# Running products in a PSUM bank: keep formed in place of the scores, one two-bank PSUM tile split in two, and a new order

## The chip, the cores and the metric

The kernel runs on one core of a Trainium2 chip. The metric is the device time of one execution in microseconds. Several engines work side by side, each with a queue of its own that it takes strictly in order: TensorE (PE) for matrix products, with its weight loads (PEld), VectorE (DVE), ScalarE (ACT), GpSimd (POOL) and SyncE (SP), which issues the DMAs. Products land in PSUM, eight banks of 512 fp32 columns in each of 128 partitions. Inputs of the other engines lie in SBUF or, except for POOL, in PSUM.

## The reference, cut to what matters

Two layers work on a sequence of 512 tokens with 1024 channels. The even layer joins a gated linear recurrence and a block attention (softmax); the odd one joins a stick-breaking attention (8 heads of 64 channels) and a state-space model. Each begins with an RMS norm and an adaptive modulation (adaLN) and ends with an output projection. The change is in the stick-breaking attention and around it:

```python
def stick_breaking_attention(q, k, v):
    for blk in range(t_ // SB_QBLOCK):                 # 4 blocks of 128 queries
        q0 = blk * SB_QBLOCK
        end = q0 + SB_QBLOCK
        z = jnp.einsum('bhqd,bhkd->bhqk', q[:, :, q0:end], k[:, :, :end]) * scale
        strict = jnp.arange(end)[None, :] < qpos[:, None]
        log_beta = jax.nn.log_sigmoid(z)
        log_keep = jnp.where(strict, jax.nn.log_sigmoid(-z), 0.0)
        later = lax.cumsum(log_keep, axis=3, reverse=True) - log_keep
        w = jnp.where(strict, jnp.exp(log_beta + later), 0.0)
        outs.append(jnp.einsum('bhqk,bhkd->bhqd', w, v[:, :, :end]))
```

A weight is thus sigmoid(z) times the product of sigmoid(-z) over all later keys.

## The kernel before, in words

The program is first recorded, then ordered, then emitted. `Rec.add` notes each operation with its operands; `Rec.cost` gives it an estimated duration; `Rec.schedule` places the operations one after another on the engine queues, by a priority (`prio`, the PE time recorded so far) that the tables `SHIFTS` shift by ranges of operation numbers (nanoseconds, negative is earlier). Operations recorded with `either` may run on DVE or on POOL or ACT; the planner gives them to the engine on which they end sooner, after the bias that `CHOICE` adds for ranges of numbers. `emit` then writes the instructions in that order, and the tile framework adds the waits between engines by what each instruction reads and writes. All instructions carry one line number, 603, so rows are told apart by the names of their tiles.

Matrix products with 512 columns are formed from a high and a low part of each factor (`mm3`: three products). A weight tile `wst` comes by DMA, ACT (or POOL) casts it to `wh`, and DVE or POOL forms the remainder `wl`.

At the start x comes in eight tiles; ACT squares them, DVE adds the squares into an accumulator (in the trace `t`), and `rms` sums its columns on PE (`ones,t`), forms the mean on DVE (`ms`), a power on POOL, a diagonal on DVE (`diag`), a product on PE, and a copy `rb`. `modulate` then forms `hs` (DVE), `hh` (ACT) and `hl` (DVE) for each of eight blocks of channels, with a scale and shift that DVE's dot products over `aw` deliver. Eight products of x with itself into a bank that nobody reads (`warm`) stand in PE's queue as well.

PSUM's banks are shared by tags: `pj` banks 0 to 3, `ps` 4 and 5, `pt` 6, `pv` 7, and in the attentions `fj` 0 and 1, `as` 2 to 4 (scores), `at` 5 and 6 (transposed weights), `av` 7 (values). `pw`, a row of 1024 columns that the dot products read early in the kernel, takes banks 6 and 7 together. For it, banks 6 and 7 are one PSUM tile of 1024 columns, and `pt`, `pv`, `at` and `av` are views of it.

In `attend`, per pair of query blocks and one or two heads: `both` spreads q into `qd` by DMA, `scores` forms the scores in an `as` bank (rows `k,qd`), `weights_moba` (even layer) or `weights_stick` (odd layer) forms the weights in SBUF, PE transposes them into an `at` bank (rows `ident,w` and `ident,u`), ACT casts that to `wth` and DVE forms the remainder `wtl`. `values` multiplies with v into the `av` bank (rows `wth,v`) and then ACT and DVE read the halves of that bank into `ya` (even) or `yb` (odd), twice each. In `weights_stick`, `u` and `keep` are two SBUF tiles of the tag `u2o`, which has six slots; five of them share memory with other temporaries. There are 24 tiles in the odd layer, 8 with two heads and 16 with one, of 128, 256, 384 and 512 columns per head, and 32 scans. While the attentions run, the output projections and, in the odd layer, a gated product (`glu`, tile `zval`) fill PE's queue.

The state-space model is worked in four quarters between the odd layer's projections; it transposes through `pt` and multiplies into `pv`.

Of the kernel before, what the change touches and what calls it, by code (L numbers as in the profile page):

```python
# [11 lines left out]
F32 = mybir.dt.float32  # L12
# [3 lines left out]
OP = mybir.AluOpType  # L16
AX = mybir.AxisListType
PSUM = bass.MemoryType.PSUM
# [164 lines left out]
class Eng:  # L183
# [8 lines left out]


SHIFTS = (
# [11 lines left out]
)  # L206
CHOICE = (
# [3 lines left out]
)  # L211


class Rec:
# [191 lines left out]
    def schedule(self, key=None):  # L406
# [14 lines left out]
        last = {}  # L421
# [13 lines left out]
        dma_free, act_set, order = 0.0, None, []  # L435

        port, port_free, tile = None, 0.0, None
        slot, speed, rows = 0, 1.0, 0.0

        def arrive(op):  # L440
            for e in [a[0] for a in op.alts] or [op.eng]:
# [35 lines left out]
        while left:  # L477
            best = None
            for e in self.ENGINES:
                now = clock[e]  # L480
                pick = None
                for op in cand[e].values():
                    r = op.ready
                    got = ()
                    if op.new:
                        s = place(op)
# [14 lines left out]
                    start = max(now, r)  # L501
                    sw = 0
                    if e == "scalar" and op.aset and act_set not in op.aset:
                        sw = 1
                    k = (start if start > now + (self.dma_window if e == "sync" else self.window) else now,
                         key[op.n] + (4000.0 if sw else 0.0), op.n)
# [8 lines left out]
            _, op, sw, got, start, e = best  # L515
# [73 lines left out]
    def emit(self, nc, base, psum, preload):  # L589
        def real(v):  # L590
            return v.real() if isinstance(v, View) else v
        for op in self.order:
            if isinstance(op, str):
                preload(op)
                continue
            for b in op.new:
                if b.psum:
                    b.ap = psum[self.banks[b.tag][b.slot] if b.tag != "pw" else 8]
                    continue
                off = base + 4 * self.memory[b.tag][0][b.slot]  # L600
                b.ap = nc.alloc_sbuf_tensor_at("%s_%d" % (b.name, op.n), list(b.shape), b.dtype, offset=off).ap()
            kw = {k: real(v) for k, v in op.kw.items() if k != "nbytes"}
            op.ins = getattr(getattr(nc, op.eng), op.method)(*[real(a) for a in op.args], **kw)  # L603
# [74 lines left out]
class Hybrid:  # L678
# [7 lines left out]
    def bank(self, tag):  # L686
        return self.R.buf([128, 512], F32, tag)
# [55 lines left out]
    def setup(self):  # L743
# [24 lines left out]
        row = R.buf([1, D], F32, "crow")  # L768
        self.act(row, crow, "Tanh", scale=0.5)
        R.vector.scalar_tensor_tensor(out=row, in0=row, scalar=1.0, in1=crow, op0=OP.add, op1=OP.mult)  # L770
        self.crow = R.buf([128, D], F32, "pw")
        for i in range(2):
            h = slice(i * 512, i * 512 + 512)
            R.tensor.matmul(self.crow[:, h], lhsT=self.ones[0:1], rhs=row[:, h], start=True, stop=True)

    def load_late(self):
        R = self.R
# [79 lines left out]
            self.either_tt(sq, sq, acc, OP.add)  # L857
        return sq

    def rms(self, acc, bank):  # L860

        R, n = self.R, acc.shape[1]
        r = n // 128
        p = self.bank(bank)
        for i in range(r):
            R.tensor.matmul(p[:, i:i + 1], lhsT=acc[:, i * 128:i * 128 + 128], rhs=self.ones[:, 0:1], start=True, stop=True)
        ms = R.buf([128, 4], F32, "st", "ms")[:, 0:r]
        R.vector.tensor_scalar(ms, p[:, 0:r], 1.0 / D, EPS, op0=OP.mult, op1=OP.add)
        R.gpsimd.tensor_tensor(out=ms, in0=ms, in1=self.mhalf[:, 40:40 + r], op=OP.pow)
        diag = R.buf([128, r, 128], F32, "t2" if n == 512 else "sq256", "diag")  # L870
        R.vector.tensor_tensor(out=diag, in0=self.ident[:, None, :].to_broadcast([128, r, 128]),
                               in1=ms[:, :, None].to_broadcast([128, r, 128]), op=OP.mult)
        p = self.bank(bank)[:, 0:n]
        diag = diag.rearrange("p r e -> p (r e)")
        R.tensor.matmul(p, lhsT=self.ones, rhs=diag, start=True, stop=True)
        return p

    def new_h(self):
# [215 lines left out]
    def weights_stick(self, s, g, n):  # L1094

        R = self.R
        w, keep = (R.buf([128, g, n], F32, "u2o", x) for x in ("u", "keep"))
        self.act(keep, s, "Sigmoid", scale=-1.0)
        self.act(w, s, "Sigmoid")
        for j in range(g):  # L1100

            z = keep[:, j, 1:n][:, ::-1]
            R.vector.tensor_tensor_scan(out=z, data0=z, data1=z, initial=1.0, op0=OP.mult, op1=OP.min)
        R.vector.tensor_tensor(out=w[:, :, 0:n - 1], in0=w[:, :, 0:n - 1], in1=keep[:, :, 1:n], op=OP.mult)
        return w

    def attend(self, q, k, v, sg, mix, weights, scratch, mask, groups):
# [94 lines left out]
    def even(self):  # L1202
# [6 lines left out]
            R.sync.dma_start(xt, A['x_t'][k * 128:k * 128 + 128, :])  # L1209
            self.x.append(xt)  # L1210
        aw0 = self.ada_load(0)

        warm = self.bank("ps")
        for k in range(8):
            R.tensor.matmul(warm[:, 0:256], lhsT=self.x[k][:, 0:128], rhs=self.x[k][:, 0:256], start=True, stop=True)
        for k in range(8):
            acc = self.square(k, everything, acc)
        ab = R.buf([128, 3, 8], F32, "ab")
        self.new_h()
        rb = R.buf([128, 512], F32, "t2", "rb")  # L1220
        R.scalar.copy(rb, self.rms(acc, "ps"))
        xl = []

        def evac_xl(b, p):
# [425 lines left out]
@with_exitstack  # L1650
def hybrid_kernel(ctx, tc, *aps):
    nc = tc.nc
    m = Hybrid(dict(zip(_NAMES, aps)), aps[len(_NAMES)])
    R = m.record()
    R.schedule()
    pool = ctx.enter_context(tc.tile_pool(name="psum", bufs=1, space=PSUM))
    psum = [pool.tile([128, 512], F32, name="bank%d" % i) for i in range(6)]
    two = pool.tile([128, 1024], F32, name="bank67")
    psum += [two[:, 0:512], two[:, 512:1024], two]
    ctx.enter_context(tc.manual_schedule())  # L1660
    R.emit(nc, -(-nc.sbuf_base // 32) * 32, psum, nc.scalar.preload_act_table_set)
    return m


# [17 lines left out]
```

## Time and profile before

| | us |
|---|---|
| median of 3 runs | 568.76 (567.86 to 572.07) |
| the profiled execution, its own time | 569.02 |
| span of the profiled execution | 567.2 |
| PE busy, share of the span | 526.4 (93%) |
| DVE busy | 461.8 (81%) |
| ACT busy | 285.6 (50%) |
| POOL busy | 156.1 (28%) |

The span runs from the first to the last instruction of the profiled execution; 1.8 us of its time lie around it. Busy times of PE are sums over pipelined products, so 93% doesn't mean that PE works at its peak. The stages follow one another with overlap: start and first projection to 64 us, the even layer's projections and recurrence to about 200, its attention and output to about 290, the odd layer's projections with the state-space quarters to about 445, its attention and output to the end. Times in rows are microseconds from the span's start unless marked ns.

### The profile page before, as it was taken

What the parts mean: (1) busy time and instruction counts of PE and PEld (TensorE: products, weight loads), DVE (VectorE), ACT (ScalarE), POOL (GpSimd) and SP (SyncE); (2) the same over time, 40 slices, a digit from 0 to 9 for tenths busy, and PEclk for the clock granted to TensorE, in tenths of its full rate; (3) what the DMA queues carried; (4) which work ended last, traced back from release to release, by engine and by line L of the source; (5) the groups of instructions that cost most, each with busy time, mean ns of one, the idle gap of its engine ahead of it and who ended that gap; (6) DMA issues with size and microseconds to landing.
All of it is one profiled execution on the core that took longest, in us unless ns stands there. A gap on an engine that the chain in (4) does not pass through costs nothing.

```text
span 567.2 us, 8032 instructions
## 1 busy us (share of the span) xinstructions
PE 526.4 (93%) x2762; PEld 426.3 (75%) x2762; DVE 461.8 (81%) x917; ACT 285.6 (50%) x551; POOL 156.1 (28%) x164
## 2 busy tenths in 40 slices
PE   6697999999999999899999998989999988999997
PEld 3465688667777777788779987867877876776787
DVE  5799998999978988879787666767865799998973
ACT  5424532484645867764652327246254675845320
POOL 0000231233435304454799000200041502212100
PEclk9999999999999999999999999999999999999999
DMA  8985599981234634311023321212025343312122
GB/s 297 404 293 184 200 342 318 373 281 55 84 112 142 157 112 141 107 43 49 27 74 106 117 75 37 75 39 68 27 82 163 91 119 90 116 28 68 44 102 86
DMA packets 45755, 75.59 MB, mean 133 GB/s; under 512 B 4241, under 2 KB 28945, under 8 KB 44690
## 3 DMA queue, kind: packets, MB, share of 16 engines
q1 hardware_dynamic: 45714, 75.08, 40.9%
q8 instruction: 22, 0.36, 0.3%
q14 instruction: 19, 0.16, 0.1%
HBM read 64.57 MB, written 2.10 MB: 118 GB/s over the span
## 4 chain that ended last, share of the span: by engine, by line
PE 49%; DVE 29%; ACT 10%; DMA 4%; issue 4%; POOL 2%; SPq 0%; DVEq 0%; ACTq 0%; POOLq 0%
PE bank L603 49%; DVE aw L603 4%; DVE wl L603 3%; DMA aw<-in_od_ada_t_dram 2%; DVE keep L603 2%; DVE wtl L603 2%; DVE hs L603 2%; POOL qms L603 2%; DVE hl L603 2%; ACT wpr_wpi_opr_opi L603 1%; DVE u L603 1%; DMA wst<-in_od_w_out_dram 1%; ACT wth L603 1%; DVE x L603 1%; DVE yb L603 1%
## 5 line engine op out<-in xcount | busy, mean ns | idle before, releaser
L603 ACT CAST wh<-wst 128x1024 fp32r<-128x1024 f32 x58 | 60.9, 1050 | 79.5 <-PE bank L603 49.1
L603 PE MATMUL bank<-wl,hh 128*128 128x512 f32 x224 | 88.2, 397 | 1.8 <-DVE wl L603 1.8
L603 PE MATMUL bank<-wh,hl 128*128 128x512 f32 x224 | 87.7, 396 | 0.2 <-DVE hl L603 0.2
L603 PE MATMUL bank<-wh,hh 128*128 128x512 f32 x224 | 87.1, 398 | 0.4
L603 DVE TENSOR_TENSOR wl<-wst,wh 128x1024 fp32r<-128x1024 f32 x53 | 67.7, 1282 | 15.0 <-ACT wh L603 14.6
L603 PE MATMUL bank<-hh,wh 128*128 128x512 f32 x160 | 61.1, 409 | 8.4 <-ACT hh L603 8.4
L603 PE MATMUL bank<-hl,wh 128*128 128x512 f32 x160 | 63.5, 404 | 0.0
L603 POOL TENSOR_TENSOR wl<-wst,wh 128x1024 fp32r<-128x1024 f32 x15 | 36.3, 2425 | 93.3 <-ACT wh L603 83.4
L603 PE MATMUL bank<-hh,wl 128*128 128x512 f32 x160 | 61.5, 393 | 0.0
L603 PEld LDWEIGHTS bank<-wl,hh 128*128 128x128 f32 x224 | 46.0, 205 | 10.6 <-DVE wl L603 3.1
L603 PEld LDWEIGHTS bank<-wh,hh 128*128 128x128 f32 x224 | 45.7, 205 | 9.7 <-issue 1.2
L603 PE MATMUL bank<-q,wh 128*128 128x256 f32 x256 | 50.6, 289 | 2.1 <-DVE q L603 0.7
L603 PEld LDWEIGHTS bank<-wh,hl 128*128 128x128 f32 x224 | 46.0, 205 | 8.2 <-DVE hl L603 0.8
L603 POOL TENSOR_TENSOR qms<-qms,derived 128x8 f32<-128x8 f32 x16 | 29.3, 1837 | 62.6 <-DVE qms L603 61.2
L603 PEld LDWEIGHTS bank<-hh,wh 128*128 128x128 f32 x160 | 29.9, 191 | 19.5 <-ACT hh L603 13.0
L603 PEld LDWEIGHTS bank<-q,wh 128*128 128x128 f32 x256 | 40.6, 190 | 4.4 <-DVE x L603 2.2
L603 DVE CUSTOM_DVE_ANT_0 aw<-aw,bank,lcols 128x1024 f32<-128x1024 f32 x32 | 40.5, 1273 | 2.4 <-DMA aw<-in_od_ada_t_dram 2.4
L603 PEld LDWEIGHTS bank<-hl,wh 128*128 128x128 f32 x160 | 30.6, 191 | 8.4 <-DVE hl L603 1.5
L603 PE MATMUL bank<-q,wl 128*128 128x256 f32 x128 | 36.2, 288 | 0.0
L603 PEld LDWEIGHTS bank<-hh,wl 128*128 128x128 f32 x160 | 30.1, 188 | 6.6 <-issue 0.7
L603 PE MATMUL bank<-k,qd 128*128 128x512 f32 (+3 forms) x128 | 34.1, 326 | 0.0
L603 ACT CAST wth<-bank 128x512 fp32r<-128x512 f32 (+2 forms) x48 | 24.0, 516 | 18.1 <-PE bank L603 15.1
(213 smaller groups left out, 1199.1 us busy)
## 6 DMA issues: line engine op xcount, KB each, us to landing
aw<-in_od_ada_t_dram SPq DMA_DIRECT2D x24, 512.0 KB, 5.9
aw<-in_ev_ada_t_dram SPq DMA_DIRECT2D x8, 1024.0 KB, 8.8
wst<-in_od_w_in_dram SPq DMA_DIRECT2D x16, 512.0 KB, 3.6
wst<-in_ev_w_in_dram SPq DMA_DIRECT2D x12, 512.0 KB, 7.2
wst<-in_ev_w_in_dram SPq DMA_DIRECT2D x24, 256.0 KB, 3.5
aw<-in_ev_gate_t_dram SPq DMA_DIRECT2D x8, 512.0 KB, 4.4
wst<-in_ev_w_out_dram SPq DMA_DIRECT2D x8, 512.0 KB, 4.2
qd<-q SPq DMA_DIRECT2D x32, 128.0 KB, 2.8
```

Of the source, the lines that this page charges most:

```text
L603: op.ins = getattr(getattr(nc, op.eng), op.method)(*[real(a) for a in op.args], **kw)
```

## The change

Four things change. In `weights_stick`, `keep` is no longer a tile: the second sigmoid overwrites the scores in their PSUM bank, the scan runs there in place with a column of ones (broadcast from SBUF) as its second input, and the product reads it there. The two sigmoids change places. The two-bank PSUM tile is kept only for `pw`, in a pool that is closed when bank 6 or 7 is first asked for; after that they are two tiles of one bank each. The eight `warm` products over x are removed; two products of constants in `setup` and two in the even layer's first `rms` are added. The tables `SHIFTS` and `CHOICE` are new, with 37 and 9 entries where there were 53 and 14, and the planner takes PE's clock as low at the start (`speed`). From the first `rms` on, an operation's number is 4 less than before.

```diff
 SHIFTS = (
-    (2018, 2019, 10518), (3854, 3894, 10778), (1287, 1298, 5289), (30, 597, 1554), (1147, 1634, 3396),
...
-    (4262, 4303, 13376), (1439, 1476, -789),
+    (3043, 3052, 8774), (1018, 1022, 3924), (1599, 1710, 5502), (1584, 1598, 4615), (2497, 2513, -6921),
+    (3049, 3072, -26458), (3231, 3550, 2254), (486, 517, 1193), (2346, 2401, -24614), (3853, 3885, 7046),
...
+    (519, 670, -2481), (2126, 2133, 2353), (3624, 3661, 1122), (1122, 1215, -435), (1644, 1663, -16577),
+    (3005, 3006, 23610), (815, 1188, 1028), (1837, 1847, 518), (3071, 3134, -9248), (702, 707, -7222),
...
 )
...
-        slot, speed, rows = 0, 1.0, 0.0
+        slot, speed, rows = 0, 0.5, 0.0
...
-                    b.ap = psum[self.banks[b.tag][b.slot] if b.tag != "pw" else 8]
+                    b.ap = psum(8 if b.tag == "pw" else self.banks[b.tag][b.slot])
...
+        warm = self.bank("ps")
+        R.tensor.matmul(warm, lhsT=self.ones, rhs=self.moba_mask, start=True, stop=True)
         self.crow = R.buf([128, D], F32, "pw")
         for i in range(2):
             h = slice(i * 512, i * 512 + 512)
             R.tensor.matmul(self.crow[:, h], lhsT=self.ones[0:1], rhs=row[:, h], start=True, stop=True)
+        R.tensor.matmul(warm, lhsT=self.ones, rhs=self.moba_mask, start=True, stop=True)
...
-    def rms(self, acc, bank):
+    def rms(self, acc, bank, warm=None):
...
+        if warm is not None:
+            R.tensor.matmul(warm, lhsT=self.ones, rhs=acc, start=True, stop=True)
...
+        if warm is not None:
+            R.tensor.matmul(warm, lhsT=self.ones, rhs=diag, start=True, stop=True)
...
-        w, keep = (R.buf([128, g, n], F32, "u2o", x) for x in ("u", "keep"))
-        self.act(keep, s, "Sigmoid", scale=-1.0)
+        w = R.buf([128, g, n], F32, "u2o", "u")
         self.act(w, s, "Sigmoid")
+        self.act(s, s, "Sigmoid", scale=-1.0)
         for j in range(g):
 
-            z = keep[:, j, 1:n][:, ::-1]
-            R.vector.tensor_tensor_scan(out=z, data0=z, data1=z, initial=1.0, op0=OP.mult, op1=OP.min)
-        R.vector.tensor_tensor(out=w[:, :, 0:n - 1], in0=w[:, :, 0:n - 1], in1=keep[:, :, 1:n], op=OP.mult)
+            z = s[:, j, 1:n][:, ::-1]
+            R.vector.tensor_tensor_scan(out=z, data0=z, data1=self.ones[:, 0:1].to_broadcast([128, n - 1]), initial=1.0,
+                                        op0=OP.mult, op1=OP.min)
+        R.vector.tensor_tensor(out=w[:, :, 0:n - 1], in0=w[:, :, 0:n - 1], in1=s[:, :, 1:n], op=OP.mult)
         return w
...
-        warm = self.bank("ps")
-        for k in range(8):
-            R.tensor.matmul(warm[:, 0:256], lhsT=self.x[k][:, 0:128], rhs=self.x[k][:, 0:256], start=True, stop=True)
...
-        R.scalar.copy(rb, self.rms(acc, "ps"))
+        R.scalar.copy(rb, self.rms(acc, "ps", self.bank("ps")))
...
-    psum = [pool.tile([128, 512], F32, name="bank%d" % i) for i in range(6)]
-    two = pool.tile([128, 1024], F32, name="bank67")
-    psum += [two[:, 0:512], two[:, 512:1024], two]
+    banks = {i: pool.tile([128, 512], F32, name="bank%d" % i) for i in range(6)}
+    first = ExitStack()
+    banks[8] = first.enter_context(tc.tile_pool(name="two", bufs=1, space=PSUM)).tile([128, 1024], F32, name="two")
+
+    def bank(i):
+
+        if i not in banks:
+            first.close()
+            pool = ctx.enter_context(tc.tile_pool(name="last", bufs=1, space=PSUM))
+            banks.update({j: pool.tile([128, 512], F32, name="bank%d" % j) for j in (6, 7)})
+        return banks[i]
```

## Rows read from the trace of the kernel before

**Rows 1.** Windows: stretch, its length, busy us of PE, PEld, DVE, ACT, POOL, clock, DMA.
```profile
22.00:64.00 42.00, 34.35 (x132) 24.99 (x133) 39.87 (x103) 14.53 (x22) 2.40 (x1) 1.00 0.70 250
200.00:262.00 62.00, 55.76 (x375) 48.08 (x373) 50.27 (x137) 41.56 (x106) 26.00 (x34) 1.00 0.30 86
480.00:540.00 60.00, 56.39 (x315) 44.79 (x313) 56.61 (x83) 34.32 (x72) 12.12 (x12) 1.00 0.22 65
```

**Rows 2.** Timeline of PE, 10 to 26 us: start, length, engine, line, what [idle before].
```profile
10.90 4.64 PE L603 MATMUL bank<-x 128*128 128x256 f32 x10
15.33 1.71 PE L603 MATMUL bank<-ones,t 128*128 128x1 f32 x8
19.13 2.07 PE L603 MATMUL bank<-diag,ones 128*128 128x512 f32 x2 [2.10 <-DVE diag L603]
23.42 2.07 PE L603 MATMUL bank<-hh,wh 128*128 128x512 f32 x4 [2.21 <-ACT hh L603]
```

**Rows 3.** Timeline of DVE in the same stretch.
```profile
10.81 1.49 DVE L603 TENSOR_TENSOR t<-t,t 128x512 f32<-128x512 f32 x2 [0.69 <-ACT t L603]
13.30 1.28 DVE L603 CUSTOM_DVE_ANT_0 aw<-aw,bank,ecols 128x1024 f32<-128x1024 f32 x1 [1.00 <-DMA aw<-in_ev_ada_t_dram]
...
17.07 0.16 DVE L603 TENSOR_SCALAR ms<-bank 128x4 f32<-128x4 f32 x1 [1.09 <-PE bank L603]
18.38 0.69 DVE L603 TENSOR_TENSOR diag<-ident,ms 128x512 f32<-128x512 f32 x1 [1.15 <-POOL ms L603]
...
21.86 0.75 DVE L603 SCALAR_TENSOR_TENSOR hs<-x,ab,rb 128x512 f32<-128x512 f32 x1 [0.51 <-ACT rb L603]
```

**Rows 4.** Who waited for whom, 200 to 262 us: total us, times, longest.
```profile
DVE ya L603 <- ACT wth L603: 3.4, 4, 1.9
...
ACT ya L603 <- DVE wtl L603: 2.5, 4, 0.9
...
ACT wth L603 <- DVE ya L603: 2.1, 2, 1.1
...
PE bank L603 <- ACT ya L603: 1.4, 3, 0.5
```

**Rows 5.** Timeline of DVE and PE, two of these waits.
```profile
225.72 0.42 DVE L603 SCALAR_TENSOR_TENSOR ya<-bank,ya 64x256 f32<-64x256 f32 x1 [0.30 <-ACT wth L603]
...
230.46 0.44 PE L603 MATMUL bank<-ident,w 128*128 128x128 f32 x2 [0.47 <-ACT ya L603]
```

**Rows 6.** Who waited for whom, 345 to 400 us.
```profile
PE bank L603 <- ACT kx_ug_yt L603: 2.7, 4, 1.6
```

**Rows 7.** Groups by shape, whole span: count | busy us, mean ns | idle before.
```profile
L603 DVE TENSOR_TENSOR wtl<-bank,wth 128x512 fp32r<-128x512 f32 x24 | 16.4, 684 | 1.1 <-PE bank L603 0.7 <-ACT wth L603 0.2
...
L603 DVE TENSOR_TENSOR_SCAN keep<-keep 128x511 f32<-128x511 f32 x8 | 10.2, 1277 | 0.0
...
L603 ACT ACTIVATE keep<-bank 128x512 f32<-128x512 f32 x12 | 7.2, 599 | 2.4 <-DVE u L603 1.8 <-PE bank L603 0.3
...
L603 DVE TENSOR_TENSOR u<-u,keep 128x511 f32<-128x511 f32 x8 | 5.5, 683 | 0.0
```

**Rows 8.** Timeline of PE and DVE, one tile of 512 columns of the odd attention.
```profile
489.45 0.62 PE L603 MATMUL bank<-k,qd 128*128 128x512 f32 x2
...
494.85 1.76 DVE L603 TENSOR_TENSOR_SCAN keep<-keep 128x511 f32<-128x511 f32 x1
...
498.01 0.69 DVE L603 TENSOR_TENSOR u<-u,keep 128x511 f32<-128x511 f32 x1
```

**Rows 9.** Waits and DVE groups, 445 to 540 us; POOL's timeline; the tile zval (min/median/max ns).
```profile
ACT keep L603 <- DVE u L603: 4.9, 7, 1.3
...
L603 DVE TENSOR_TENSOR wl<-wst,wh 128x1024 fp32r<-128x1024 f32 x9 | 10.9, 1211 | 0.2 <-ACT wh L603 0.2
...
474.35 2.50 POOL L603 TENSOR_TENSOR wl<-wst,wh 128x1024 fp32r<-128x1024 f32 x1
...
L603 DVE SCALAR_TENSOR_TENSOR zval<-zval,sgs x4: 681/950/2807, 463.1 to 498.6; 128x512 f32<-128x512 f32 x4
```

More of the change, by code (lines that the diff above doesn't have):

```diff
@@ L194 @@
 SHIFTS = (
[11 rows of a table removed]
[8 rows of a table added]
 )
 CHOICE = (
[3 rows of a table removed]
+    (2594, 2626, -1252), (438, 517, 666), (2023, 2030, 493), (2111, 2197, -4241), (634, 736, 2066), (3652, 3707, 728),
+    (3792, 3897, 3536), (2146, 2211, 3242), (2437, 2552, 1411),
 )
@@ L1656, in hybrid_kernel @@
     pool = ctx.enter_context(tc.tile_pool(name="psum", bufs=1, space=PSUM))
-    psum = [pool.tile([128, 512], F32, name="bank%d" % i) for i in range(6)]
-    two = pool.tile([128, 1024], F32, name="bank67")
-    psum += [two[:, 0:512], two[:, 512:1024], two]
+    banks = {i: pool.tile([128, 512], F32, name="bank%d" % i) for i in range(6)}
[7 more added lines that the diff above has]
+        return banks[i]
     ctx.enter_context(tc.manual_schedule())
-    R.emit(nc, -(-nc.sbuf_base // 32) * 32, psum, nc.scalar.preload_act_table_set)
+    R.emit(nc, -(-nc.sbuf_base // 32) * 32, bank, nc.scalar.preload_act_table_set)
     return m
```

16 rows, old and new, of tables (CHOICE, SHIFTS) are left out of this document.

## The prediction

> **What bounds the kernel now.** I read the windows of the span first, then the timeline of the first 25 us, then who waited for whom in the attention stages, then single rows of the timeline. The windows [rows 1] show two different regimes. From 22 to 64 us VectorE (DVE) is busy 39.87 of 42.00 us: the adaLN dot products set the pace, whatever TensorE (PE) does. In the even layer's attention (200 to 262) no engine is full: PE is busy 55.76 of 62.00 us, DVE 50.27, ScalarE (ACT) 41.56, so the end is set by engines handing work to each other. In the odd layer's attention (480 to 540) DVE is again close to the limit, 56.61 of 60.00 us, with PE at 56.39. Outside of these PE streams 512-column matmuls back to back; the change doesn't touch that work, so its worth must come from the start, from the two attentions and from the state-space quarters.
>
> **Start: the warm-up matmuls move.** Before, eight fp32 matmuls of 256 columns over x stand in PE's queue, and the five that are left at 10.90 occupy PE until 15.5 us [rows 2]. The sum of squares that they have nothing to do with is complete on DVE at 10.81 + 1.49 = 12.30 us [rows 3], but its column sums start on PE only at 15.33 [rows 2]. DVE then waits for them and for what follows: 1.09 us before ms at 17.07, 1.15 before diag at 18.38, 0.51 before hs at 21.86 [rows 3], 2.75 us in all. Removing the x matmuls lets the column sums start at 12.3, 3.0 us earlier. From ms to hs the old chain takes 21.86 - 17.07 = 4.79 us; it now starts at about 14.1, but hs also needs the scale of block 0, whose data lands at 13.30 [rows 3] and whose two dots hold DVE until about 16.0, so diag waits for DVE until 16.0 instead of 15.4. That puts hs at 16.0 + (21.86 - 18.38) = 19.5, a gain of 2.4 us. From there DVE is the limit up to 64 us [rows 1], so the head start is passed on; DMA is at 0.70 of its time in that stretch, enough in hand.
> The four added matmuls have 512 columns in fp32, like the diag product, which took 2.07 us [rows 2]. The two in setup need only constants and fit before 12.3 us, where PE now does the x matmuls. The two in rms stand behind the column sums and behind the diag product, where PE was idle 2.10 and 2.21 us [rows 2] while POOL, DVE and ACT worked; each fits by 0.03 to 0.14 us, and if the cover is gone, each costs up to 2.07 us less what is left of the gap. I cost them at nothing. [...] I expect no gain from the clock. Term: -2.4 us, bounds -3.0 and 0.
>
> **Two one-bank tiles.** Banks 6 and 7 are views of one tile, and the rows show that accesses to one wait for accesses to the other. At 230.46 PE's transposes of w wait for ACT writing ya; they have no data in common, ya is read out of the values' bank (7) and the transposes write banks 5 and 6. At 225.72 DVE's ya waits for ACT's wth, again only bank 7 against bank 6 [rows 5]. Each such pair turns two independent evacuations into one chain. In 200 to 262 us these kinds of waits come to 3.4 + 2.5 + 2.1 + 1.4 = 9.4 us of engine time [rows 4]. Not all of it reaches the end: they overlap, and the values bank has one slot, so PE still waits for the last ya of a pair. PE was idle only 62.00 - 55.76 = 6.24 us there [rows 1]. What is late next is DVE with 50 of 62 us. I take a third, -3.0 us, bounds 0 and -6.2. The state-space quarters use the same two banks; PE waits 2.7 us there for ACT's Kx copies [rows 6], part of which is true data; I take a quarter, -0.7, bounds 0 and -2.7. The closing of the two-bank pool waits for the last reader of crow, which the old order already did for the same banks: nothing.
>
> **Stick attention.** Per tile the operations stay: two sigmoids on ACT, a scan per head, one product on DVE; 24 tiles, 32 scans. What changes is where keep lies. The price of a scan from PSUM is in no row; the nearest are a 511-column product with both inputs in SBUF at 683 ns and a 512-column subtraction with one input in PSUM at 684 ns [rows 7], so I cost the scan at its present 1277 ns and the product at 683. [...]
> [...]
> The order of the sigmoids turns round: before, the scan could start behind the first, 0.60 us [rows 7], while the second ran; now it waits for both. That is 0.6 us of latency per tile, hidden as long as DVE has other work ready: it waited 3.4 us in the 60 us [rows 1]. On the other side a tile needs one slot of u2o, not two; ACT waited 4.9 us for DVE to give slots back [rows 9]. And scan and product each have one SBUF tensor input less. That matters to POOL: at 474.35 POOL formed a wl for 2.50 us, and DVE's zval product, two SBUF inputs, took its longest, 2.81 us, beside it, where its fastest takes 0.68 [rows 9]. A scan that doesn't take part in this lets POOL run beside it. Nine wl of this stretch are on DVE, 1.21 us each [rows 9]; the planner gives one to POOL if it ends sooner there. I take -2.0 us for slots, bank waits and POOL together, bounds -8 and +15 (the last is worked out below).
>
> **The new order.** SHIFTS and CHOICE are replaced whole. Among the moves that can be placed are 26 us earlier for a group of q/k projection matmuls of the odd layer, 25 us earlier for ones beside its first state-space quarter, 26 us earlier for the last output matmuls, 17 us earlier for one values step of the even attention, and 24 us later for a state-space output. Weight loads, their casts on ACT and their remainders on DVE or POOL follow these, past the qd copies in SP's queue. No row prices an order that was not run; I take 0 with bounds of 4 us either way.
>
> **Sum.** -2.4 - 3.0 - 0.7 - 2.0 + 0 = -8.1 us. The profiled execution took 569.02 us, its span 567.2; it is 0.26 us above the median of 568.76. 569.0 - 8.1 = 560.9, against the median 560.7: I say 561. A measurement of this kernel tells about 1% from no change, so faster begins below 563.1 and slower above 574.4.
>
> **Rivals.**
> *Off the path.* The waits named are real, but other chains end as late: DVE's total work in the odd attention is unchanged, and the even attention keeps its single values bank. Then the start gives 1.4 us and the attentions 1 us: 566.5. For it: DVE 56.6 of 60 us; against it: in 200 to 262 no engine is full.
> *The scores' bank is held too long (slower).* There are three banks for scores. In one tile the scores are written at 489.45, the scan follows at 494.85 and the product at 498.01 [rows 8], if they are taken in the order of the queue. Before, the bank was free after the second sigmoid; from now on it is held to 498.70, 9.25 us, 0.6 more with the turned order. Sixteen such tiles in 60 us make 3.75 us a tile, so three banks allow 11.2 us. The rival decides once DVE puts about one more tile's work (scan 1.28, product 0.68, wtl 0.68) and a wl (1.21) ahead of a product: 13.7 us of hold, 2.5 too many, a third of it per tile, 0.83 x 16 = 13 us of PE standing at the head of its queue with every projection and output matmul behind it. Without the 2.0 of this stage: 569.0 - 6.1 + 13 = 576. For it: the hold is already 83% of what is allowed; against it: the slots of u2o held no more than three tiles in flight before either.
> *More than the sum.* If scans and products leave the shared path to POOL, five of the nine wl move there, 6.0 us off a DVE that is the limit, and the even attention gives its whole 6: 569.0 - 2.4 - 6 - 0.7 - 8 = 552. [...]
> *It doesn't do what it says*: the scan runs slower from PSUM. [...]
>
> **How the numbers follow.** The forecast 0.47, off the path 0.28, more than the sum 0.13, bank held 0.08, slow scan 0.04. The forecast's own range is 556 to 565. Faster: nearly all of the forecast and the large gain, 0.57; same 0.33; slower 0.10. The range reaches from 551 to 571: it leaves out the bank's case, the slow scan's end and half a tail of the large gain.
>
> **What would show it.** In the profile after: column sums of t at about 12.3 us instead of 15.33 and hs before 20 us; no wait of ident transposes for ya or yb, and none of ya for wth; scans of 511 columns within 60 ns of 1.28 us; no wait of the first sigmoid for u; DVE's wl fewer in the odd attention and POOL's more; PE not waiting for DVE's u ahead of its scores. The prediction is wrong if DVE's scans are longer, if PE's waits before k,qd grow, or if the new order gives back elsewhere (64 to 200 or 290 to 445 us, where nothing is changed) what the stages gain.

## The result, and the profile after

The changed kernel takes 554.83 us in the median of 4 runs (551.43 to 556.52), the kernel before 569.42 in the runs beside it: a ratio of 0.9732, 95% interval 0.9668 to 0.9796. It is faster, by 14.6 us where 8 were forecast: inside the range of 551 to 571, but 1.2 us below the forecast's own 556 to 565. The profiled execution took 551.43 us, its span 549.7; it is the fastest of the four, so leads read from it are some 3 us larger than those of the medians.

The start first. Timelines of PE and of DVE in the kernel after, in the form of [rows 2] and [rows 3]:

```profile
11.92 1.87 PE L599 MATMUL bank<-ones,t 128*128 128x1 f32 x8 [4.33 <-DVE t L599]
13.65 2.06 PE L599 MATMUL bank<-t,ones 128*128 128x512 f32 x2
16.09 3.59 PE L599 MATMUL bank<-diag,ones 128*128 128x512 f32 x4 [0.38 <-DVE diag L599]
20.43 0.96 PE L599 MATMUL bank<-hh,wh 128*128 128x512 f32 x3 [0.76 <-ACT hh L599]
```

```profile
13.95 0.16 DVE L599 TENSOR_SCALAR ms<-bank 128x4 f32<-128x4 f32 x1
...
15.35 0.68 DVE L599 TENSOR_TENSOR diag<-ident,ms 128x512 f32<-128x512 f32 x1
...
18.87 0.75 DVE L599 SCALAR_TENSOR_TENSOR hs<-x,ab,rb 128x512 f32<-128x512 f32 x1 [0.57 <-ACT rb L599]
```

The column sums begin at 11.92 us, not 15.33, and hs at 18.87, not 21.86. DVE no longer waits ahead of ms and diag. The warm-up products over t and diag lie where PE was idle. The first products over hh run faster than before, three in 0.96 us where four took 2.07 in [rows 2].

Windows of the kernel after, two of the start and the stretches of [rows 1], with the same columns:

```profile
10.00:18.00 8.00, 5.70 (x13) 3.09 (x14) 6.91 (x12) 2.89 (x4) 1.03 (x1) 0.50 1.02 406
...
20.00:22.00 2.00, 1.57 (x6) 1.16 (x7) 1.59 (x2) 0.38 (x1) 0.00 (x0) 1.00 0.99 406
...
22.00:64.00 42.00, 35.01 (x141) 25.19 (x140) 40.79 (x111) 17.12 (x27) 2.66 (x1) 1.00 0.73 265
...
200.00:262.00 62.00, 59.04 (x404) 53.30 (x405) 55.51 (x132) 38.35 (x89) 29.79 (x35) 0.97 0.31 91
...
480.00:540.00 60.00, 58.29 (x380) 51.39 (x379) 47.75 (x74) 25.75 (x56) 22.35 (x19) 1.00 0.25 75
```

Both attentions end earlier in the kernel after (see the tiles below), so the last two windows no longer hold the same work. From the odd attention's first product u to the end of its last, before and after:

```profile
453.90:546.40 92.50, 85.70 (x490) 69.20 (x490) 86.52 (x136) 51.22 (x108) 17.61 (x16) 1.00 0.29 83
```

```profile
447.20:521.60 74.40, 72.22 (x411) 58.91 (x409) 71.87 (x119) 49.19 (x105) 30.41 (x25) 1.00 0.32 89
```

The granted clock is 0.50 from 10 to 18 us, while PE works at the sums and the warm-up, 0.66 from 18 to 20 and 1.00 from 20 to 64. From 200 to 262 us PE is idle 2.96 us instead of 6.24, the last 9 us of it behind the attention. From 480 to 540 DVE is busy 47.75 us instead of 56.61, but that window now holds 19 us behind the last u. From the first u to the last, DVE's work has fallen from 86.52 to 71.87 us and POOL's has grown from 17.61 to 30.41; DVE (97% of the stretch) and PE (97%) are both close to full, so DVE is still a limit there.

Who waited for whom in the kernel after, 200 to 262 us, PE's, DVE's and ACT's waits of the kinds in [rows 4]:

```profile
ACT ya L599 <- DVE ya L599: 4.0, 5, 1.3
...
DVE wtl L599 <- ACT wth L599: 1.9, 4, 1.1
...
DVE ya L599 <- ACT ya L599: 1.2, 1, 1.2
```

These are true dependences, or one slot's. The four kinds of [rows 4], 9.4 us of engine time (DVE's ya for wth, ACT's ya for wtl, wth for ya, PE for ACT's ya), no longer appear in the list of the stretch, and with them go the two of [rows 5]. In the state-space quarters, 345 to 400 us, the wait of [rows 6] has fallen from 2.7 us to 0.6:

```profile
PE bank L599 <- ACT kx_ug_yt L599: 0.6, 1, 0.6
```

Stick attention's groups by shape after, in the form of [rows 7], and the remainders wl between 437 and 540 us, which answer to [rows 9]:

```profile
L599 DVE TENSOR_TENSOR_SCAN bank<-bank,ones 128x511 f32<-128x511 f32 x8 | 9.7, 1217 | 1.2 <-ACT bank L599 1.1
...
L599 DVE TENSOR_TENSOR u<-u,bank 128x511 f32<-128x511 f32 x8 | 5.4, 676 | 0.0
...
L599 POOL TENSOR_TENSOR wl<-wst,wh 128x1024 fp32r<-128x1024 f32 x7 | 16.7, 2393 | 0.3
...
L599 DVE TENSOR_TENSOR wl<-wst,wh 128x1024 fp32r<-128x1024 f32 x4 | 5.0, 1258 | 0.5 <-ACT wh L599 0.4
```

Scan and product cost no more from PSUM than from SBUF (1217 against 1277 ns, 676 against 683). POOL forms 7 of the wl there, DVE 4; before it was 9 on DVE and one on POOL in the nearest stretch, 445 to 540.

To follow the gain through the stages I use three tiles: qn's first product stands behind the start and the first of the even layer's projections, the last ya ends the even attention, the last qn stands ahead of most of the odd attention, and the last product u ends its weights. Tiles ya, qn and u of the kernel before (count, ns min/median/max, first to last start, shape):

```profile
L603 DVE SCALAR_TENSOR_TENSOR ya<-bank,ya x16: 416/422/428, 201.8 to 259.5; 64x256 f32<-64x256 f32 x16
...
L603 DVE TENSOR_TENSOR qn<-bank,qms x16: 673/692/694, 152.3 to 452.7; 128x512 f32<-128x512 f32 x16
...
L603 DVE TENSOR_TENSOR u<-u,keep x24: 414/668/868, 453.9 to 545.7; 128x383 f32<-128x383 f32 x8, 128x511 f32<-128x511 f32 x8, 128x254 f32<-128x254 f32 x4, 128x510 f32<-128x510 f32 x4
```

and of the kernel after:

```profile
L599 DVE SCALAR_TENSOR_TENSOR ya<-bank,ya x16: 404/422/429, 198.8 to 252.6; 64x256 f32<-64x256 f32 x16
...
L599 DVE TENSOR_TENSOR qn<-bank,qms x16: 672/692/693, 148.0 to 445.4; 128x512 f32<-128x512 f32 x16
...
L599 DVE TENSOR_TENSOR u<-u,bank x24: 404/607/685, 447.2 to 520.9; 128x383 f32<-128x383 f32 x8, 128x511 f32<-128x511 f32 x8, 128x254 f32<-128x254 f32 x4, 128x510 f32<-128x510 f32 x4
```

The lead is 4.3 us at the first qn, 6.9 at the last ya, 7.3 at the last qn, 24.8 at the last u and 17.5 at the end (567.2 against 549.7): the odd attention ends much earlier, and part of that is output work which then still has to be done behind it.

### The profile page after: what moved, and what is told of

The parts are those of the page before. It is cut to its first block, busy times and chain, and to the rows that moved or that the text cites. A ratio compares the mean times of both kernels' runs of the same rounds, so it can differ in the third digit from the quotient of the medians.

```text
span 549.7 us, 8041 instructions
## 1 busy us (share of the span) xinstructions
PE 517.5 (94%) x2754; PEld 422.6 (77%) x2754; DVE 456.4 (83%) x945; ACT 281.2 (51%) x545; POOL 155.0 (28%) x142
## 4 chain that ended last, share of the span: by engine, by line
PE 56%; DVE 23%; ACT 8%; issue 5%; DMA 5%; POOL 2%; SPq 1%; DVEq 0%; ACTq 0%; POOLq 0%
PE bank L599 56%; DVE aw L599 4%; DVE wl L599 3%; DMA aw<-in_od_ada_t_dram 3%; ACT wh L599 1%; DMA aw<-in_ev_ada_t_dram 1%; DVE bank L599 1%; SPq L599 1%; POOL wl L599 1%; DVE wtl L599 1%; DVE q L599 1%; ACT wpr_wpi_opr_opi L599 1%; DVE hs L599 1%; ACT hh L599 1%; DVE xl L599 1%
## 5 line engine op out<-in xcount | busy, mean ns | idle before, releaser
L599 POOL TENSOR_TENSOR wl<-wst,wh 128x1024 fp32r<-128x1024 f32 x23 | 57.9, 2523 | 138.5 <-ACT wh L599 132.9
L599 PE MATMUL bank<-wh,hh 128*128 128x512 f32 x224 | 86.0, 395 | 2.4 <-DVE sga L599 1.3
L599 DVE TENSOR_TENSOR wl<-wst,wh 128x1024 fp32r<-128x1024 f32 x45 | 56.7, 1262 | 6.5 <-ACT wh L599 4.6
L599 DVE CUSTOM_DVE_ANT_0 aw<-aw,two,lcols 128x1024 f32<-128x1024 f32 x32 | 40.5, 1275 | 4.1 <-DMA aw<-in_od_ada_t_dram 4.1
L599 DVE SCALAR_TENSOR_TENSOR x<-bank,ab,x 128x256 f32<-128x256 f32 (+1 forms) x48 | 26.8, 567 | 14.5 <-PE bank L599 14.4
L599 PE MATMUL bank<-k,qd 128*128 128x128 f32 (+3 forms) x128 | 33.6, 331 | 0.0
```

## Experiments

My theory after the result was the prediction's third rival: POOL beside the scans brings the surplus in the odd attention. Against it stood the split of the two-bank tile, sized at 3.7 us, and the new order, sized at 0. Each ratio below is against runs of the kernel before on the same chip (medians 570.1 to 570.8 us).

**The split alone, on the kernel before** (split_before):

```diff
...
-    two = pool.tile([128, 1024], F32, name="bank67")
-    psum += [two[:, 0:512], two[:, 512:1024], two]
...
+            first.close()
+            pool = ctx.enter_context(tc.tile_pool(name="last", bufs=1, space=PSUM))
+            banks.update({j: pool.tile([128, 512], F32, name="bank%d" % j) for j in (6, 7)})
...
```

> The kernel before with one edit: banks 6 and 7 are two one-bank tiles; every instruction and its order stay as before. If the waits across the two banks are on the path (the prediction's terms for the even attention and the state-space quarters), -3.0 - 0.7 gives about 565.3 us, ratio 0.993, and the last ya comes about 3 us earlier. If other chains end as late, 568 us or more, ratio 0.998 to 1.002. If the odd attention gains as well, below 563.

559.81 us, ratio 0.9802 (0.9750 to 0.9853): a gain of 10.3 us by the medians and 11.3 by the ratio, almost three times the prediction's two terms, with not one instruction moved. Its trace tells where. Tiles ya, qn and u:

```profile
L603 DVE SCALAR_TENSOR_TENSOR ya<-bank,ya x16: 402/422/428, 202.1 to 256.8; 64x256 f32<-64x256 f32 x16
...
L603 DVE TENSOR_TENSOR qn<-bank,qms x16: 670/691/693, 153.2 to 448.5; 128x512 f32<-128x512 f32 x16
...
L603 DVE TENSOR_TENSOR u<-u,keep x24: 411/668/871, 449.7 to 537.8; 128x383 f32<-128x383 f32 x8, 128x511 f32<-128x511 f32 x8, 128x254 f32<-128x254 f32 x4, 128x510 f32<-128x510 f32 x4
```

Its first qn is 0.9 us later than before. From there it gains 3.6 us up to the last ya (2.7 of lead), 1.5 up to the last qn (4.2), 3.7 up to the last u (7.9) and 0.7 more to the end (558.6 against 567.2). So the even attention is near its term of 3.0, the stretch with the state-space quarters gives twice their 0.7, and 4.4 us come from the odd attention, where the two banks hold the transposes of u and the values.

**The two-bank tile put back into the changed kernel** (unsplit_after): the same edit the other way, every instruction and its order as after.

> The changed kernel with the two-bank tile put back; every instruction and its order stay as after. If the split is what the new order rests on, the loss is at least the two terms of the prediction, 3.7 us, and up to 8 us, since the running products in PSUM now lie in banks 5 to 7 as well: 558 to 563 us, ratio 0.983 to 0.990 against the kernel before. If the split matters little, 554 to 556, ratio 0.973 to 0.977.

570.77 us, ratio 1.0015 (0.9979 to 1.0050): the whole gain is gone, 15.9 us, more than I had allowed for. The new order on the two-bank tile is no better than the old one, although the start and the products in PSUM are in it. One thing in the expectation is wrong: the running products lie in the scores' banks, 2 to 4, and not in 5 to 7.

**By stage** (odd_joined, even_joined, even_attention_joined): the changed kernel in its own order, with one two-bank tile in a part of it, made by closing one pool of PSUM and opening the next where neither bank is in use.

```diff
+    def anew(joined, name):
+        stack.close()
+        last = stack.enter_context(tc.tile_pool(name=name, bufs=1, space=PSUM))
+        if joined:
+            two = last.tile([128, 1024], F32, name="bank67")
+            banks.update({6: two[:, 0:512], 7: two[:, 512:1024]})
+        else:
+            banks.update({j: last.tile([128, 512], F32, name=name + str(j)) for j in (6, 7)})
```

> The changed kernel, same instructions in the same order; banks 6 and 7 are two tiles as after, but become one two-bank tile at the odd layer's attention. The whole two-bank tile cost some 15 us (570.8 against about 555). If the cross-bank waits cost by stage in proportion to the leads that the trace of that kernel lost (9 us by the last ya, 5 more by the last odd qn, 5 more to the end), this one costs 4 to 6 us: 559 to 561. If the odd attention has the larger share because running products and transposes of u now stand in line behind each other, 563 or more. By the prediction, which gave the odd attention at most a part of 2 us, under 557.

Here the tile is joined from the odd attention's first bank 6 or 7 on. 555.96 us, 0.9754 (0.9708 to 0.9800): within the intervals no loss. In its trace the last qn comes 1.1 us earlier than after (444.3), the span ends 3.5 later (553.2), so the odd attention lost 4.6 us in that execution. The medians are 1.1 us apart, which is the expectation's last case, a loss inside the term of 2.0. On top of the tile joined everywhere else it costs 5.0 us (570.77 against 565.77, below). Its size in the new order is thus open between 1 and 5 us.

> The counterpart: same instructions and order, one two-bank tile through the even attention and the state-space quarters, two tiles from the odd layer's attention on. By the leads lost in the trace of the kernel with the two-bank tile kept, 9 to 14 us: 564 to 569. By the prediction's terms, 3.0 + 0.7: 559. If waits earlier in the kernel are taken up by slack behind them, under 559, and the two stages' costs don't add up to 15.

Joined up to there, split from there on. 565.77 us, 0.9912 (0.9883 to 0.9941), 10.9 us over the changed kernel, within what the leads gave.

> The changed kernel, same instructions in the same order; one two-bank tile through the even layer's attention alone, two tiles from the state-space quarters on. The kernel joined through both took 565.8 us (ratio 0.991), the changed one about 555 (0.973). In its trace the lead was lost by 9.5 us up to the last ya (262.1 against 252.6) and by 5 more up to the last odd qn. If these losses are each stage's own, this one gives 562 to 563.5 (ratio 0.985 to 0.988); if the quarters only pass on what the attention lost, 565; by the prediction's term for the even attention, 558.

Joined up to the first values of the state-space quarters. 561.84 us, 0.9830 (0.9783 to 0.9877), 7.0 us over the changed kernel by the medians; the quarters cost the 3.9 us between it and the one before. Its tiles ya and qn:

```profile
L599 DVE SCALAR_TENSOR_TENSOR ya<-bank,ya x16: 407/422/428, 199.5 to 260.9; 64x256 f32<-64x256 f32 x16
...
L599 DVE TENSOR_TENSOR qn<-bank,qms x16: 673/691/693, 146.8 to 454.2; 128x512 f32<-128x512 f32 x16
```

The first qn is 1.2 us earlier than in the kernel after and the last ya 8.3 later: 9.5 us are lost in the even attention, and 8.8 still stand at the last qn and at the end (558.5 against 549.7). Nothing behind it takes them up. Of the four kinds of [rows 4] three are back in its waits from 200 to 262 us, and PE waits for wtl longer than after (0.9 us):

```profile
PE bank L599 <- ACT ya L599: 2.0, 1, 2.0
...
PE bank L599 <- DVE wtl L599: 1.3, 3, 0.5
...
ACT ya L599 <- DVE wtl L599: 0.9, 1, 0.9
...
DVE ya L599 <- ACT wth L599: 0.7, 2, 0.4
```

The longest is PE's: at 215.57 its transposes of w, which go to banks 5 and 6, wait 1.97 us for ACT, which reads ya out of bank 7.

```profile
215.57 0.76 PE L599 MATMUL bank<-ident,w 128*128 128x128 f32 x5 [1.97 <-ACT ya L599]
```

These waits alone are not the 9.5 us. Windows of this kernel, and one of the kernel after:

```profile
203.50:206.00 2.50, 2.50 (x9) 2.10 (x8) 1.18 (x5) 2.01 (x6) 1.07 (x2) 0.50 0.38 92
217.00:220.00 3.00, 3.00 (x10) 2.42 (x9) 2.84 (x6) 0.76 (x2) 0.73 (x1) 0.50 0.12 46
```

```profile
200.00:253.00 53.00, 51.76 (x358) 46.48 (x358) 47.30 (x112) 34.58 (x83) 25.76 (x33) 1.00 0.33 97
```

Behind PE's pauses (0.67 us ahead of 200.69 and 0.52 ahead of 202.42, then the 1.97) the granted clock is 0.50 for some 3.4 us each time, and products of 512 columns take 0.63 us instead of 0.39; in the kernel after it is 1.00 from 200 to 253 us. Two stretches of 3.4 us at half the clock are 3.4 us of PE's work, my estimate of what the clock adds at most. In even_joined the quarters, from the last ya to the last qn, take 4.8 us longer than here (460.2 - 262.1 against 454.2 - 260.9). By stage the split is thus worth 9.5, 4.8 and 4.6 us in the traces of the new order, 19 together, which is the difference of the spans with the tile whole and split (569.0 and 549.7). By the medians it is 7.0, 3.9 and 1.1 to 5.0, together 12 to 16.

**The products in PSUM alone, on the kernel before** (stick_alone; the diff is that of weights_stick):

> The kernel before with the running products in PSUM alone; the two-bank tile, start and tables stay. By the prediction's term, 566.8. If the products help only where the transposes and the values can use their banks independently, 568 to 571. If the scores' banks are held too long (the slower rival), 573 or more, with PE waiting for DVE's u ahead of scores.

567.22 us, 0.9954 (0.9921 to 0.9987): 3.6 us by the medians and 2.6 by the ratio, near the term of 2.0. PE's weight loads wait for u 0.5 us at most, and no product of PE does; the slower rival doesn't show.

**Both of these on the kernel before** (split_stick):

> The kernel before with two edits, the two one-bank tiles and the running products in PSUM; start and tables as before. The split alone gave 559.8. If the products in PSUM are worth what their removal cost the changed kernel, 4 to 5 us, 555 to 556; if the old order can't use them, 559 to 560. Against the changed kernel with old tables (557.3) it shows what the new start is worth: by the prediction 2.4 us, so about 559.5 if that holds.

559.63 us, 0.9813 (0.9764 to 0.9863), but its runs fall into two groups, three from 556.1 to 558.0 and three from 561.3 to 562.0. The profiled one is of the upper group: its first qn starts at 157.3, though up to there it is the same program as split_before, whose first qn is at 153.2. Where those 4 us come from I didn't settle. From the first qn to the end it takes 402.2 us (559.5 - 157.3), split_before 405.4: the products gain 3.2 us there. By the medians they give nothing on top of the split (559.63 against 559.81). What the start is worth can't be read from this run's median either.

**The old order** (old_tables): the changed kernel with the old SHIFTS and CHOICE, their operation numbers moved to the same operations.

```diff
-    (3043, 3052, 8774), (1018, 1022, 3924), (1599, 1710, 5502), (1584, 1598, 4615), (2497, 2513, -6921),
...
+    (2014, 2015, 10518), (3850, 3890, 10778), (1283, 1294, 5289), (25, 593, 1554), (1143, 1630, 3396),
...
```

> The changed kernel with the old SHIFTS and CHOICE, renumbered to the same operations; everything else as after, so the planner places the work anew. The prediction's sum gave the order 0 with 4 us either way: 551 to 559. If the search for the order carries the surplus over the sum (14.6 measured, 8 forecast), 561 to 566 us, ratio 0.985 to 0.995, with the odd attention as late as before. If the running products in PSUM carry it (POOL free to form wl), 555 to 558 and the odd attention keeps its lead.

557.30 us, 0.9763 (0.9717 to 0.9808): 2.5 us over the changed kernel, intervals overlapping. The search doesn't carry the surplus by itself. In the trace the start loses with the old order: hs begins at 20.5, not 18.9, because wl waits 1.53 us for ACT ahead of it; the last of the eight hs is at 60.2, half a microsecond earlier than before, and the first qn at 152.1 against 152.3.

**keep in SBUF again** (keep_sbuf): the changed kernel with weights_stick as before.

```diff
...
+        self.act(keep, s, "Sigmoid", scale=-1.0)
...
-        self.act(s, s, "Sigmoid", scale=-1.0)
...
```

> The changed kernel with weights_stick as before (keep in SBUF, two slots of u2o a tile); new tables, one-bank tiles and the new start stay. If the surplus comes from scans and products that read at most one SBUF tensor and leave POOL to run (the rival called more than the sum), the odd attention gives back most of the 10 us that it gained between its projections and the end: 562 to 566 us, ratio 0.985 to 0.995. By the prediction's own term for stick attention, 2.0 us are lost: 557, ratio 0.977. If it is worth nothing, 555.

560.33 us, 0.9814 (0.9767 to 0.9862): 5.5 us over the changed kernel, between the two expectations. Scans in its timeline of DVE, each by itself, and what POOL does beside the second row:

```profile
491.05 0.95 DVE L599 TENSOR_TENSOR_SCAN keep<-keep 128x383 f32<-128x383 f32 x1
...
493.51 3.14 DVE L599 TENSOR_TENSOR_SCAN keep<-keep 128x383 f32<-128x383 f32 x1
...
502.96 1.22 DVE L599 TENSOR_TENSOR_SCAN keep<-keep 128x511 f32<-128x511 f32 x1
```

```profile
493.16 2.67 POOL L599 TENSOR_TENSOR wl<-wst,wh 128x1024 fp32r<-128x1024 f32 x1 [0.59 <-ACT wh L599]
```

A scan of 383 columns, 0.95 us when POOL is quiet (another at 500.59, with POOL idle from 495.83 to 512.09, takes the same), takes 3.14 us when it begins beside a wl that ends at 495.83. The mean of 1277 ns in [rows 7] holds such collisions too: the scan of [rows 8] took 1.76 us beside a product of POOL that ends at 495.53, an undisturbed one of 511 columns takes 1.22, as from PSUM. In the kernel after a scan of 511 columns begins beside the same work of POOL and takes its 1.20 us:

```profile
496.36 1.20 DVE L599 TENSOR_TENSOR_SCAN bank<-bank,ones 128x511 f32<-128x511 f32 x1
```

```profile
495.79 2.40 POOL L599 TENSOR_TENSOR wl<-wst,wh 128x1024 fp32r<-128x1024 f32 x1
```

There the scan's only SBUF input is the column of ones. Over the stage the scans of 511 and 383 columns cost DVE 4.7 us more in keep_sbuf than after (means 1476 against 1217 ns and 1278 against 954, eight of each). The planner of keep_sbuf gives POOL only 2 wl from 437 to 540 us, where it gives 7 after.

**wl kept off POOL** (wl_on_vector): the changed kernel, where wl of the odd attention and output is formed on DVE alone.

```diff
...
-        self.less(lo, st, hi)
+        if self.on_vector:
+            R.vector.tensor_tensor(out=lo, in0=st, in1=hi.bitcast(F32), op=OP.subtract)
+        else:
+            self.less(lo, st, hi)
...
+        self.on_vector = True
...
```

> The changed kernel with the weights' remainders wl of the odd layer's attention and output formed on DVE alone (POOL formed 7 of them); the planner places the rest. If the products in PSUM gain because POOL can form wl beside the scans, this gives back most of the 5 us that the kernel with keep in SBUF lost: 559 to 561. Seven times 1.21 us on DVE, 8.5 us, is the most that can come back. If the gain is the slots of u2o, 555 to 556.5.

558.17 us, 0.9777 (0.9731 to 0.9823): 3.3 us over the changed kernel by the medians, 2.6 by the ratios, about half of what keep_sbuf loses, and less than expected; its interval overlaps that of the changed kernel. All 11 wl of the stage are now on DVE. From the first u to the end of the last:

```profile
446.80:521.60 74.80, 69.05 (x381) 53.74 (x381) 73.49 (x125) 50.61 (x106) 6.32 (x8) 1.00 0.28 74
```

The last u is no later than in the kernel after (520.9 in both). What is lost lies behind it: PE has done 69.05 us of work by then instead of 72.22, and the output products that are left make the end 6.3 us later in the traces (556.0 against 549.7).

**Half the slots** (half_slots):

```diff
-    m["u2o"] = spare + [e], 512
+    m["u2o"] = spare[:3], 512
```

> The changed kernel with three slots of u2o instead of six, so as many tiles in flight as before, and keep still in PSUM. If the gain of stick attention is the slots (ACT waited 11.3 us for DVE's u to give slots back in the kernel with keep in SBUF), most of its 5 us come back: 558 to 561. If it is POOL beside the scans, 555 to 556.5.

550.98 us, 0.9646 (0.9604 to 0.9688): no loss, so slots are not what the products in PSUM give. It is the fastest median of all, 3.9 us under the changed kernel on another chip, but the two intervals overlap and the traces agree within 1.5 us at every stage (last ya 251.2, last qn 444.2, last u 519.9, end 548.4). ACT waits for DVE's u nowhere in the stage, where it waits 11.3 us in keep_sbuf, which has as many tiles in flight. Whether half_slots is faster than the changed kernel stays open.

**No warm-up matmuls** (no_warm): the four are taken out, none put in their place.

```diff
...
-        warm = self.bank("ps")
-        R.tensor.matmul(warm, lhsT=self.ones, rhs=self.moba_mask, start=True, stop=True)
...
-            R.tensor.matmul(warm, lhsT=self.ones, rhs=acc, start=True, stop=True)
...
```

> The changed kernel without the four warm-up matmuls and with none over x either; the tables are renumbered to the same operations. The prediction says that these matmuls cost nothing and that no clock is gained on the path, since DVE sets the pace from 22 to 64 us: 555, ratio within 0.003 of the changed kernel. If the higher clock from 20.4 us on is worth something, the first real matmuls run at half pace again for 2 to 4 us, and up to 2 us are lost: 557. If the warm-up matmuls delay the column sums or diag, 1 us is won.

554.51 us, 0.9717 (0.9669 to 0.9764): the same as the changed kernel. PE's products over hh now run slower up to 25.4 us (records of 0.63 us, 0.39 from 25.75 on), but the second hs is 0.55 us later than in the kernel after (24.30 against 23.75), and the first one was already 0.56 later (19.43 against 18.87): DVE sets the pace, and PE's rate there costs nothing. The trace has one accident of its own, DVE's timeline at 32 us:

```profile
31.90 2.85 DVE L599 SCALAR_TENSOR_TENSOR hl<-hs,ab,hh 128x512 fp32r<-128x512 f32 x1
```

POOL's wl begins at 31.85, 0.05 us ahead of this hl with two SBUF inputs, which then takes 2.85 us instead of 0.75, to 0.55 us past the end of wl at 34.20. In the kernel after wl begins at 31.30, when hl is already running, from 30.95 on, and hl takes 0.74 us.

## Why the prediction was right, and where it was too small

*Start.* The chain up to hs was right and a little small: hs is 3.0 us earlier where 2.4 were forecast, the last of the eight (57.3 against 60.7) 3.4. Its steps hold: the column sums start with the end of t, diag behind the two dots. I had diag at 16.0 and it is at 15.35. That the warm-up costs nothing is shown by no_warm, and that a faster PE there gives nothing is too. I expected no gain from the clock; PE's faster rate did come some six microseconds earlier, at 20.4 us instead of about 26, and it gave nothing: 554.83 us with the warm-up, 554.51 without. That the head start is passed on is not shown for the new start by itself: with the old tables 1.4 us at the first hs are 0.5 at the last and 0.2 at the first qn. No run has the old start, or the planner's old `speed`, in the new order.

*Two one-bank tiles.* This is the step that failed in size: -3.0 and -0.7 stood for what measures -10.3 on the kernel before. The mechanism was the right one, and its share in the even attention (3.6 us by the trace) was near. Two things were missing. I put the odd attention's waits between the two banks into a joint 2.0 for "slots, bank waits and POOL together", without rows of their own, and they gave 4.4 by the trace on the old order (1 to 5 in the new one). And I took the bound of 6.2 us from the PE idle time of the old order; the new order loses 9.5 us there with the tile whole, some of it, by my estimate above, at a granted clock of 0.50, which no term had. The planner's code books the two banks as separate in both kernels, so it could never see these waits, and an order can pay for them without knowing.

*Stick attention.* -2.0 against 2.6 by the ratio when done alone; right. In the changed kernel it is worth 5.5 us (keep_sbuf). About half of that is wl on POOL (wl_on_vector, with overlapping intervals), none of it is slots (half_slots); the rest I take to be the scans' own collisions with POOL, 4.7 us of DVE's time in the trace of keep_sbuf, which no run isolates. ACT's wait for DVE to give back slots, 4.9 us in [rows 9], was therefore DVE being late, not a want of slots. A PSUM source costs no more in the groups above: 1217 ns a scan of 511 columns against 1277 from SBUF (1.22 us undisturbed), 676 a product against 683. Beside POOL's wl the scan in PSUM took 1.20 us, where one of 383 columns in SBUF took 3.14 instead of 0.95. No trace shows what DVE and POOL share there, only these times.

*Order.* 0 with 4 us either way, measured 2.5 by the medians with all else in place, intervals overlapping. But on the two-bank tile the same tables are worse than the old ones: stick_alone has a ratio of 0.9954 without the new start, unsplit_after 1.0015 with it, 3.5 us apart before the start is counted.

*Rivals.* Off the path (566.5) fell with split_before. The bank held too long (576) fell with stick_alone; after, PE waits once for DVE's u, 1.7 us, and that is ahead of the transposes of u, not of scores. The slow scan fell with 1217 ns: no run shows a scan that is slower from PSUM, so nothing measured stands for the slow scan's end that the range leaves out. More than the sum (552) came nearest to the time, 2.8 us off where the forecast was 6.2 off, and partly by luck: POOL's share is some 3 us and not 6, the even attention gave 3.6 on the kernel before and not 6, and the bank waits of the odd attention and most of those of the quarters, which make up for it, were not in it. It had 0.13.

## What to carry to other kernels

Two buffers that are views of one tile are one buffer to whatever inserts the waits: count the waits that a tile boundary makes in every stage that uses it, with a row for each stage, before sizing the split, and test it alone, since it moves no instruction (here it gave 10.3 us). A bound from idle time holds for the order in which it was read; a new order can need the freedom more than the old one used it (here a bound of 6.2 us, and 9.5 lost). An operation moved so that it reads one SBUF tensor instead of two may gain little itself and yet leave the engine beside it to work (here the scan's mean went from 1277 to 1217 ns, and POOL forms 7 wl in the stage where it forms 2 with keep in SBUF). And a window that holds a stage before the change may hold the next stage after it: compare from event to event.

## What was not expected of the hardware

Two DVE operations with two inputs in SBUF lost more than their own length beside one POOL wl: 2.85 us instead of 0.75 for hl, 3.14 instead of 0.95 for a scan of 383 columns. PE's products of 512 columns ran at their faster rate (records of 0.39 us) from 20.4 us on with the four warm-up products, from 25.4 with none (0.63 until then), and from about 26 with the products over x (four in 2.07 us at 23.42, four in 1.09 at 26.80), which had kept PE busy until 15.5; it gave nothing, since DVE, busy 40.79 of 42.00 us from 22 to 64, set the pace. In no_warm and in the kernel before the granted clock reads 1.00 from 10 to 30 us all the same; the lower rate shows in the records alone. In the even attention of even_attention_joined the clock fell to 0.50 twice behind pauses of PE of 0.5 to 2 us, for some 3.4 us each time; in the kernel after a pause of 0.91 us ahead of 208.23 was not followed by a fall (1.00 from 200 to 253 us).
